# Moving the token-major steps of a two-layer decoder's down projection, and its transposes

## Chip, core and metric

The kernel runs on one core of a Trainium2 chip. The metric is the device time of one launch in microseconds (us). Three executions of the kernel before took 2107.92, 2093.62 and 2107.99 us (median 2107.92). A fourth was profiled and took 2093.35 us. One program is launched, and the host only lays data out.

## What is computed

A decoder trunk of two layers on 256 tokens and a model width of 2048, all in float32:

```python
for l in range(DEPTH):                      # 2 layers
    h = rms_norm(x, norm1_g[l])
    q, k, v, gu, gv = jnp.split(h @ w_in[l], splits, axis=-1)      # 2048 x 5120
    attn = dilated_attention(rotary(q), rotary(k), v)              # 8 heads
    gm = chunked_gmlp(gelu(gu), gelu(gv), ...)                     # 8 groups
    x = x + concat(attn, gm) @ w_out[l]                            # 2048 x 2048
    h2 = rms_norm(x, norm2_g[l])
    x = x + square(relu(h2 @ w_up[l])) @ w_down[l]                 # 2048 x 8192, 8192 x 2048
return rms_norm(x, final_g)
```

## The kernel before

**Data.** The residual stream `x` and the normalised stream `hs` lie channel-major in on-chip memory: channels on the partitions, 16 chunks of 128 channels, 256 tokens along the free axis. Every matrix product is made of three matmuls on float32 values that are split into a high and a low part: high x high, low x high, high x low. A weight tile (128 x 1024, 512 KB) is loaded by SyncE into `raw` (6 buffers), ScalarE makes its high part `hi` (line 152, 7 buffers), VectorE its low part `lo` (line 162, 6 buffers).

**Steps.** The program is a list `steps`, written out in order by the Python code; TensorE runs them in that order. Three kinds of step matter.

- A *channel-major step* (`transposed`, lines 380 to 384) uses one weight tile as the stationary operand and 256 tokens as the moving one: 24 matmuls of 256 columns. In the up projection (`w_up`) four of them finish 256 hidden channels, and `after_up` then runs on VectorE and ScalarE (lines 715, 716, 611, 612). In the down projection two of them finish 256 output channels, and `update` adds them to `x` (line 471). In the last eighth `update` also makes the next norm's inputs: in layer 0 the scaled copies into `hs` (line 269 on ScalarE, 273 on VectorE), in both layers the squares (line 282, added up by line 286), in layer 1 a scaling of `x` (line 290).
- A *token-major step* (`fast`, lines 408 to 411) does part of the down projection's first 512 output channels: tokens are the stationary operand and the weights move. It works by the seven products of a Strassen-Winograd scheme: a `Top` and a `Bottom` tile are loaded, and two `Sums` tiles (upper and lower) are made from them on VectorE (lines 205, 206 and 202, 203) before they are split. It has 42 matmuls of 256 columns, in the order: top (6), bottom (12), upper (12), lower (12). Its stationary operands come from the hidden tile `half` and from `shared`, which holds sums of the hidden tile's blocks (`sums`, lines 729 to 732, and four `parts`, lines 611 and 612).
- An *input step* (`natural`, lines 431 to 433) does part of the input projection with the weights moving: 12 matmuls of 512 columns. Each layer begins with 16 of them.

**Eighths.** The hidden width of 8192 is worked off in eight pieces of 1024. Piece e is made by 16 up steps; the 12 channel-major down steps of piece e-1 follow them; and the two token-major down steps of piece e-1 stand among the up steps of piece e. The loop has a ninth round (`e == 8`) that has no up steps: the two token-major steps stand among its 12 down steps. I call the rounds with token-major steps eighths 1 to 8 and number their steps from 0. Before, the token-major steps stood behind steps 3 and 7 of an eighth (behind steps 2 and 5 in eighth 8). In eighth 1 no down steps come in between: the up steps of piece 1 follow those of piece 0 at once.

**What follows the last token-major step.** Their seven products stay in four PSUM banks through all eight eighths. `combine` (lines 744 to 751, VectorE but for the first) adds them up, two `turn_back` calls transpose the blocks on TensorE (line 760, four transposes each), and each is followed by an `update` of channels 0 to 255 and 256 to 511. In layer 0 these make `hs` chunks 0 to 3, the first that the next layer's first step reads. In layer 1 their squares go into the final norm's sum (line 297 on TensorE sums it over the channels, lines 320 to 331 make its root, line 305 spreads it, line 877 scales the output).

**Order of side work.** `later(delay, cost, fn)` puts work into a first-in first-out queue with the earliest step at which it may run; `now` counts weight tiles, and a token-major step counts as four. After each step `run_queue` runs entries that are due until a budget of 1.2 is spent; `flush` at the end runs what is left. Each step first issues the splits of tiles up to five ahead, then its matmuls, then its `after` work, then one helping of the queue. VectorE and ScalarE run what is issued strictly in that order.

Of the kernel before, what the change touches and what calls it, by code (L numbers as in the profile page):

```python
# [83 lines left out]
def trunk(ctx: ExitStack, tc: tile.TileContext, layout, xT, consts, gains, w, b_sp, w_sp, out):  # L84
# [40 lines left out]
    def aux_bank():  # L125
        return paux.tile([P, 512], F32, name="aux", tag="aux")
# [100 lines left out]
    def later(delay, cost, fn):  # L227

        queue.append((now[0] + delay, cost, fn))
# [109 lines left out]
    steps = []  # L339
# [5 lines left out]
    def collect(fn, *args, **kw):  # L345
        n = len(steps)
        fn(*args, **kw)
        part = steps[n:]
        del steps[n:]
        return part  # L350
# [92 lines left out]
    def from_tiles(tiles, n):  # L443
        return lambda k: tiles[k // n][0][:, k % n, :, :]
# [21 lines left out]
    def update(norm, c, ps, final, last):  # L466

        alone = last and final and c == KC - 2
        for j in range(2) if alone else [slice(0, 2)]:
            xj = x[:, c + j, :] if alone else x[:, c:c + 2, :]  # L470
            vec.tensor_tensor(xj, xj, ps[j][:, 0:S] if alone else pair(ps)[:, j, :], op=OP.add)  # L471
        if final:
            if not last:
                norm.chunks(c)
            norm.square(c, alone)
            if last:
                norm.gain(c)

    def layer(l, n1, n2, n3, last):
# [230 lines left out]
        def after_up(e):  # L710
            def f(c, ps):
                if hid[e][0] is None:
                    new_half(hid[e])
                z = inner[:, c // P:c // P + 2, :]
                vec.tensor_tensor(z, pair(ps), n2.R[:, None, :].to_broadcast([P, 2, S]), op=OP.mult)  # L715
                vec.scalar_tensor_tensor(z, z, 0.0, z, op0=OP.max, op1=OP.mult)  # L716
                to_half(hid[e][0], c // P, z)
                if c == 768:
                    summed[0] = False
                    if e == 0:  # L720
                        new_shared(F32R)
                        sum_parts[0] = shared[0].rearrange("p (k h t) -> p k h t", k=NH, h=2)
                    later(1, 1.5, sums)
            return f
# [16 lines left out]
        def combine():  # L741
            p1, p2, p3, p5, p7, p6, p4 = (banks[n // 2][:, n % 2 * 256:n % 2 * 256 + 256] for n in range(7))
            b1, u, c11, c12, c21, c22 = (blocks[:, n, :] for n in range(6))
            act.activation(b1, p1, AF.Copy)
            vec.tensor_tensor(u, b1, p6, op=OP.add)
            vec.tensor_tensor(c11, b1, p2, op=OP.add)
            vec.tensor_tensor(c22, u, p7, op=OP.add)
            vec.tensor_tensor(u, u, p5, op=OP.add)
            vec.tensor_tensor(c12, u, p3, op=OP.add)
            vec.tensor_tensor(c21, c22, p4, op=OP.subtract)  # L750
            vec.tensor_tensor(c22, c22, p5, op=OP.add)
            later(1, 1.5, lambda: turn_back(0, c11, c21))
            later(1, 1.5, lambda: turn_back(2, c12, c22))

        def turn_back(c, first, second):
            ps = aux_bank()
            for j in range(2):
                for tt, src in enumerate((first, second)):
                    o = j * S + tt * P
                    pe.transpose(ps[:, o:o + P], src[:, j * P:(j + 1) * P], ident)  # L760
            later(0, 1.5, lambda: update(n3, c, ps, True, last))
# [3 lines left out]
        for e in range(9):  # L765
            up, down, quick = [], [], []
            if e < 8:
                up = collect(transposed, "w_up", l, 0, KC, e * 1024, 1024, from_hs, after_up(e))
            if e:
                down = collect(transposed, "w_down", l, (e - 1) * 1024, 8, FAST, D - FAST, from_tiles([hid[e - 1]], NH),  # L770
                               lambda c, ps, e=e: update(n3, (c + FAST) // P, ps, e == 8, last), apart=last and e == 8)
                quick = collect(fast, "w_down", l, (e - 1) * 1024, 0, [hid[e - 1]], banks, e == 1, e == 8,
                                lambda: later(1, 1.5, combine))
            rest = up or down
            n = len(quick) + 1
            for i in range(n):
                steps.extend(rest[len(rest) * i // (n + 1):len(rest) * (i + 1) // (n + 1)] if quick else rest)
                steps.extend(quick[i:i + 1])
            if quick:
                steps.extend(rest[len(rest) * n // (n + 1):])  # L780
            if up:
                steps.extend(down)
        if last:
# [11 lines left out]
    for l in range(DEPTH):  # L795
        layer(l, norms[2 * l], norms[2 * l + 1], norms[2 * l + 2], l == DEPTH - 1)
# [74 lines left out]
    n = norms[-1]  # L871
# [43 lines left out]
```

## Time and profile before

| | |
|---|---|
| profiled execution | 2093.35 us |
| its span on the core | 2091.5 us (1.85 us lie around it) |
| other executions | 2093.62, 2107.92, 2107.99 us |
| TensorE (PE) busy | 2066.8 us, 99% |
| VectorE (DVE) busy | 1464.4 us, 70% |
| ScalarE (ACT) busy | 1008.9 us, 48% |
| DMA engines | 55.6% for the weight queue, 189 GB/s over the span |

In the profile's rows PE is TensorE's matmuls, PEld its weight loads, DVE VectorE, ACT ScalarE. A timeline row gives the start, the duration, the engine, the line, the operation, output and inputs, a count, and in brackets the idle time of the engine ahead of it with what ended it. A matmul's duration (0.28 us) is longer than its distance from the next one, since matmuls overlap; the distance between starts is what counts. A row of the waits gives the engine and line that waited, what it waited for, the total, the count and the longest. A row of windows gives each engine's busy time in a stretch and `PEclk`, the clock that was granted to TensorE as a share of full speed.

### The profile page before, as it was taken

The numbers are of one execution on the slowest core, as the hardware profiler recorded it, in microseconds if no ns is written. First come the engines' busy times: TensorE is split into PE (matmuls) and PEld (weight loads), VectorE is DVE, ScalarE is ACT, GpSimd is POOL, SyncE is SP. The second block draws the span as 40 slices with busy tenths as digits, with TensorE's granted clock in tenths as the row PEclk, the third lists the DMA queues.
The fourth block names the chain that finished last, engine by engine and source line by source line (L and its number), as shares of the span: only waits on it lengthen the run. The fifth ranks groups of instructions, "written<-read, shape, count | busy, mean of one in ns | idle before, by whom it ended". The sixth has DMA issues, their size and how long they took to land. (4 is left out here: it accounts for less than half of the span.)

```text
span 2091.5 us, 40406 instructions
## 1 busy us (share of the span) xinstructions
PE 2066.8 (99%) x17066; PEld 2028.3 (97%) x17066; DVE 1464.4 (70%) x1800; ACT 1008.9 (48%) x1265; POOL 68.7 (3%) x90
## 2 busy tenths in 40 slices
PE   9999999999999999999999999999999999999997
PEld 8998999899999999999989999998999999999997
DVE  7666766777677677776856576667676676777666
ACT  7555454444454444544645554545353444444444
POOL 0002300000000000000000050000000000000000
PEclk9999999999999999999999999999999999999998
DMA  8555555365565655656565556555565655556543
GB/s 320 175 172 177 196 183 191 134 225 190 172 218 178 226 192 169 216 182 201 189 204 172 183 172 197 185 181 173 170 207 177 216 188 178 196 178 216 191 162 111
DMA packets 112118, 395.38 MB, mean 189 GB/s; under 512 B 12352, under 2 KB 16448, under 8 KB 111936
## 3 DMA queue, kind: packets, MB, share of 16 engines
q1 hardware_dynamic: 110800, 389.86, 55.6%
q8 instruction: 133, 2.18, 0.4%
q10 hardware_dynamic: 1136, 2.94, 0.4%
q14 instruction: 49, 0.40, 0.1%
HBM read 390.65 MB, written 2.10 MB: 188 GB/s over the span
## 5 line engine op out<-in xcount | busy, mean ns | idle before, releaser
L152 ACT ACTIVATE hi<-raw 128x1024 fp32r<-128x1024 f32 (+1 forms) x773 | 783.7, 1046 | 420.8 <-PE acc L384 194.5
L162 DVE TENSOR_TENSOR lo<-raw,hi 128x1024 fp32r<-128x1024 f32 (+1 forms) x773 | 907.8, 1211 | 42.0 <-ACT hi L152 25.8
L380 PE MATMUL acc<-hs,hi 128*128 128x256 f32 x2816 | 784.3, 279 | 0.0
L384 PE MATMUL acc<-hs,hi 128*128 128x256 f32 x2816 | 781.8, 278 | 0.0
L382 PE MATMUL acc<-hs,lo 128*128 128x256 f32 x2816 | 781.8, 278 | 0.0
L380 PE MATMUL acc<-half,hi 128*128 128x256 f32 x2048 | 569.5, 278 | 0.0
L382 PE MATMUL acc<-half,lo 128*128 128x256 f32 x2048 | 569.1, 278 | 0.0
L384 PE MATMUL acc<-half,hi 128*128 128x256 f32 x2048 | 569.0, 278 | 0.0
L380 PEld LDWEIGHTS acc<-hs,hi 128*128 128x128 f32 x2816 | 532.3, 189 | 0.4 <-issue 0.2
L382 PEld LDWEIGHTS acc<-hs,lo 128*128 128x128 f32 x2816 | 528.8, 188 | 0.4 <-issue 0.2
L384 PEld LDWEIGHTS acc<-hs,hi 128*128 128x128 f32 x2816 | 528.6, 188 | 0.0
L380 PEld LDWEIGHTS acc<-half,hi 128*128 128x128 f32 x2048 | 387.6, 189 | 0.0
L382 PEld LDWEIGHTS acc<-half,lo 128*128 128x128 f32 x2048 | 384.4, 188 | 0.1
L384 PEld LDWEIGHTS acc<-half,hi 128*128 128x128 f32 x2048 | 384.4, 188 | 0.0
L611 ACT ACTIVATE half<-ar 128x512 fp32r<-128x512 f32 x72 | 45.6, 633 | 323.5 <-DVE ar L716 308.9
L471 DVE TENSOR_TENSOR x<-x,acc 128x512 f32<-128x512 f32 (+1 forms) x113 | 76.7, 680 | 174.6 <-PE acc L384 174.6
L715 DVE TENSOR_TENSOR ar<-acc,nR 128x512 f32<-128x512 f32 x64 | 44.2, 691 | 196.0 <-PE acc L384 196.0
L431 PE MATMUL acc<-hi,hs 128*128 128x512 f32 x256 | 101.4, 396 | 0.5 <-ACT hs L269 0.5
L433 PE MATMUL acc<-hi,hs 128*128 128x512 f32 x256 | 100.8, 394 | 0.0
L432 PE MATMUL acc<-lo,hs 128*128 128x512 f32 x256 | 100.1, 391 | 0.0
L612 DVE TENSOR_TENSOR half<-ar,half 128x512 fp32r<-128x512 f32 x72 | 49.8, 692 | 50.3 <-ACT half L611 50.3
L408 PE MATMUL aux<-hi,shared 128*128 128x256 f32 x256 | 73.4, 287 | 10.4 <-ACT shared L611 10.4
(127 smaller groups left out, 1548.2 us busy)
## 6 DMA issues: line engine op xcount, KB each, us to landing
raw<-in_w SPq DMA_DIRECT2D x731, 512.0 KB, 4.5
raw<-in_w SPq DMA_DIRECT2D x10, 256.0 KB, 5.3
x<-in_xT SPq DMA_DIRECT2D x7, 256.0 KB, 5.6
out<-x SPq DMA_DIRECT2D x7, 256.0 KB, 3.1
shared<-in_b_sp ACTq DMA_DIRECT2D x2, 512.0 KB, 7.0
shared<-in_w_sp ACTq DMA_DIRECT2D x2, 512.0 KB, 8.5
con<-in_consts ACTq DMA_DIRECT2D x1, 512.0 KB, 7.4
x<-in_xT ACTq DMA_DIRECT2D x1, 256.0 KB, 4.2
```

The costliest lines, as they stand in the source:

```text
L152: act.activation(self.h[:, j * m:(j + 1) * m], self.raw[:, j * m:(j + 1) * m], AF.Copy)
L162: vec.tensor_tensor(lo[:, r], self.raw[:, r], self.h[:, r].bitcast(F32), op=OP.subtract)
L380: pe.matmul(o, lhsT=hi, rhs=xs[:, 0, :], start=(k0 + k == 0 and (two or cb == 0)), stop=False, skip_group_check=True)
L382: pe.matmul(o, lhsT=wt.lo[:, k, cb * P:(cb + 1) * P], rhs=xs[:, 0, :], start=False, stop=False, skip_group_check=True)
L384: pe.matmul(o, lhsT=hi, rhs=xs[:, 1, :], start=False, stop=last, skip_group_check=True)
L408: pe.matmul(o, lhsT=xh, rhs=hi, start=(first and p == 0 and k == 0 and n % 2 == 0), stop=False, skip_group_check=True)
L431: pe.matmul(ps, lhsT=xh, rhs=hi, start=(k0 + k == 0), stop=False)
L432: pe.matmul(ps, lhsT=xh, rhs=lo, start=False, stop=False)
L433: pe.matmul(ps, lhsT=xl, rhs=hi, start=False, stop=(k0 + k == KC - 1))
L471: vec.tensor_tensor(xj, xj, ps[j][:, 0:S] if alone else pair(ps)[:, j, :], op=OP.add)
L611: act.activation(t[:, c:c + 2, 0, :], src, AF.Copy)
L612: vec.tensor_tensor(t[:, c:c + 2, 1, :], src, t[:, c:c + 2, 0, :].bitcast(F32), op=OP.subtract)
```

## The change

The two token-major steps now stand ahead of steps 6 and 7 of an eighth, so that one channel-major step lies between them; in eighth 1 they stand ahead of steps 10 and 11. The two `turn_back` calls become due one weight tile later. Matmuls, splits, loads and buffers are the same in kind and number.

```diff
-            later(1, 1.5, lambda: turn_back(0, c11, c21))
-            later(1, 1.5, lambda: turn_back(2, c12, c22))
+            later(2, 1.5, lambda: turn_back(0, c11, c21))
+            later(2, 1.5, lambda: turn_back(2, c12, c22))
...
             rest = up or down
-            n = len(quick) + 1
-            for i in range(n):
-                steps.extend(rest[len(rest) * i // (n + 1):len(rest) * (i + 1) // (n + 1)] if quick else rest)
-                steps.extend(quick[i:i + 1])
-            if quick:
-                steps.extend(rest[len(rest) * n // (n + 1):])
+            at = (10, 11) if e == 1 else (6, 7)
+            for i, one in enumerate(rest):
+                if quick and i in at:
+                    steps.append(quick.pop(0))
+                steps.append(one)
```

VectorE's order in eighth 1, from the last `after_up` of piece 0 on. L175 is the low part of the first token-major step's top tile, L729 to L732 begin the sums of the hidden tile, and L612 with `shared` stores a part of them. Before:

```order
L612 TENSOR_TENSOR half<-ar,half 128x2x256
L175 TENSOR_TENSOR lo<-raw,hi 128x512
L729 TENSOR_TENSOR ar<-ar 128x4x128
L730 TENSOR_TENSOR ar<-ar 128x4x128
L731 TENSOR_TENSOR ar<-ar 128x4x128
L732 TENSOR_TENSOR ar<-ar 128x4x128
L205 TENSOR_TENSOR raw<-raw 128x2x256
L206 TENSOR_TENSOR raw<-raw 128x2x256
L162 TENSOR_TENSOR lo<-raw,hi 128x1024
L612 TENSOR_TENSOR shared<-ar,shared 128x2x256
```

Now, from the same place:

```order
L612 TENSOR_TENSOR shared<-ar,shared 128x2x256
L162 TENSOR_TENSOR lo<-raw,hi 128x1024
L612 TENSOR_TENSOR shared<-ar,shared 128x2x256
L162 TENSOR_TENSOR lo<-raw,hi 128x1024
L175 TENSOR_TENSOR lo<-raw,hi 128x512
L205 TENSOR_TENSOR raw<-raw 128x2x256
L206 TENSOR_TENSOR raw<-raw 128x2x256
```

These are the last two of the four `shared` parts: all four now stand ahead of the first token-major step's splits, where before the splits were issued in between.

VectorE's order at the end of layer 0, from the `update` of down step 9 on. `x<-x,acc` is an update by a channel-major step, `x<-x,aux` one by a transposed block. Before:

```order
L471 TENSOR_TENSOR x<-x,acc 128x512
L273 SCALAR_TENSOR_TENSOR hs<-x,cols,hs 128x256 x2
L286 TENSOR_TENSOR nacc<-nacc,nsq 128x512
L471 TENSOR_TENSOR x<-x,aux 128x512
L273 SCALAR_TENSOR_TENSOR hs<-x,cols,hs 128x256 x2
L286 TENSOR_TENSOR nacc<-nacc,nsq 128x512
L162 TENSOR_TENSOR lo<-raw,hi 128x1024
L471 TENSOR_TENSOR x<-x,aux 128x512
L273 SCALAR_TENSOR_TENSOR hs<-x,cols,hs 128x256 x2
L286 TENSOR_TENSOR nacc<-nacc,nsq 128x512
L162 TENSOR_TENSOR lo<-raw,hi 128x1024
L471 TENSOR_TENSOR x<-x,acc 128x512
```

Now:

```order
L471 TENSOR_TENSOR x<-x,acc 128x512
L273 SCALAR_TENSOR_TENSOR hs<-x,cols,hs 128x256 x2
L286 TENSOR_TENSOR nacc<-nacc,nsq 128x512
L162 TENSOR_TENSOR lo<-raw,hi 128x1024 x2
L471 TENSOR_TENSOR x<-x,acc 128x512
L273 SCALAR_TENSOR_TENSOR hs<-x,cols,hs 128x256 x2
L286 TENSOR_TENSOR nacc<-nacc,nsq 128x512
L471 TENSOR_TENSOR x<-x,aux 128x512
L273 SCALAR_TENSOR_TENSOR hs<-x,cols,hs 128x256 x2
L286 TENSOR_TENSOR nacc<-nacc,nsq 128x512
L471 TENSOR_TENSOR x<-x,aux 128x512
```

Both updates by transposed blocks moved from ahead of the update of down step 11, the layer's last, to behind it.

VectorE's order at the end of layer 1, from the same place on. L321 begins the final norm's root. Before:

```order
L471 TENSOR_TENSOR x<-x,acc 128x512
L286 TENSOR_TENSOR nacc<-nacc,nsq 128x512
L471 TENSOR_TENSOR x<-x,aux 128x512
L286 TENSOR_TENSOR nacc<-nacc,nsq 128x512
L471 TENSOR_TENSOR x<-x,aux 128x512
L286 TENSOR_TENSOR nacc<-nacc,nsq 128x512
L471 TENSOR_TENSOR x<-x,acc 128x256 x2
L321 TENSOR_SCALAR rv<-aux 128x2
```

Now:

```order
L471 TENSOR_TENSOR x<-x,acc 128x512
L286 TENSOR_TENSOR nacc<-nacc,nsq 128x512
L471 TENSOR_TENSOR x<-x,acc 128x256 x2
L471 TENSOR_TENSOR x<-x,aux 128x512
L286 TENSOR_TENSOR nacc<-nacc,nsq 128x512
L471 TENSOR_TENSOR x<-x,aux 128x512
L286 TENSOR_TENSOR nacc<-nacc,nsq 128x512
L321 TENSOR_SCALAR rv<-aux 128x2
```

The update of the last down step (in two halves) moved from behind the two updates by transposed blocks to ahead of them.

## The prediction, as made before the changed kernel ran

> **What bounds the kernel now.** I read the page's first part, then TensorE's waits, then its timeline.
>
> ```profile
> span 2091.5 us, 40406 instructions
> PE 2066.8 (99%) x17066; PEld 2028.3 (97%) x17066; DVE 1464.4 (70%) x1800; ACT 1008.9 (48%) x1265; POOL 68.7 (3%) x90
> ...
> PE aux L408 <- ACT shared L611: 10.4, 2, 5.2
> ...
> PE aux L760 <- DVE ar L750: 1.1, 1, 1.1
> ```
>
> TensorE is never without work but for some 15 us of named waits. The largest is the first token-major step of eighth 1, once in each layer: it waits 5.2 us for `shared`. So the time is made of three things: these waits, the speed of TensorE behind them, and the distance between matmuls everywhere else. The next rows are the starts of that token-major step and of the step behind it, in layer 0 and layer 1, then TensorE's clock.
>
> ```profile
> 388.21 0.28 PE L408 MATMUL aux<-hi,half 128*128 128x256 f32 x1
> ...
> 401.37 0.28 PE L380 MATMUL acc<-hs,hi 128*128 128x256 f32 x1
> ...
> 1417.02 0.28 PE L408 MATMUL aux<-hi,half 128*128 128x256 f32 x1
> ...
> 1429.55 0.28 PE L380 MATMUL acc<-hs,hi 128*128 128x256 f32 x1
> ```
>
> ```profile
> 393.90:400.70 6.80, 5.78 (x25) 5.49 (x26) 6.33 (x7) 5.89 (x8) 0.00 (x0) 0.50 0.53 166
> 1421.40:1428.20 6.80, 4.46 (x19) 4.17 (x20) 6.07 (x8) 5.03 (x7) 0.00 (x0) 0.50 0.48 150
> ```
>
> The two steps last 13.16 and 12.53 us. The second fence's column before the last two is the granted clock: 0.50 for 6.8 us around the end of each wait, so that the wait costs more than its 5.2 us.
>
> The third thing is hidden in the 99%. These are starts of whole runs of matmuls in an eighth of layer 0 and one of layer 1: token-major step, channel-major steps, token-major step, channel-major steps, next token-major step.
>
> ```profile
> 482.92 0.28 PE L408 MATMUL aux<-hi,half 128*128 128x256 f32 x1
> ...
> 487.68 0.28 PE L380 MATMUL acc<-hs,hi 128*128 128x256 f32 x1
> ...
> 498.99 0.28 PE L408 MATMUL aux<-hi,half 128*128 128x256 f32 x1
> ...
> 503.94 0.28 PE L380 MATMUL acc<-hs,hi 128*128 128x256 f32 x1
> ...
> 569.23 0.28 PE L408 MATMUL aux<-hi,half 128*128 128x256 f32 x1
> ```
>
> ```profile
> 1513.05 0.28 PE L408 MATMUL aux<-hi,half 128*128 128x256 f32 x1
> ...
> 1518.00 0.28 PE L380 MATMUL acc<-hs,hi 128*128 128x256 f32 x1
> ...
> 1528.89 0.28 PE L408 MATMUL aux<-hi,half 128*128 128x256 f32 x1
> ...
> 1533.65 0.28 PE L380 MATMUL acc<-hs,hi 128*128 128x256 f32 x1
> ...
> 1601.50 0.28 PE L408 MATMUL aux<-hi,half 128*128 128x256 f32 x1
> ```
>
> In layer 0 the 576 matmuls of the long stretch take 65.29 us, 113.35 ns each, and the 96 between the two token-major steps 11.31 us, 117.8 ns each. In layer 1 it is the other way round: 67.85 us or 117.8 ns in the long stretch, 10.89 us or 113.4 ns between. The same holds in the other eighths. So the distance has two values, narrow and wide, 4.45 ns apart; it is kept until a token-major step ends and is the other one behind it (a token-major step itself runs at the distance that it found: 4.76 or 4.95 us). Up to eighth 1 both layers run narrow. In layer 0 the wide stretch stayed between the two steps; in layer 1 the wait in eighth 1 left the phase turned round, and the long stretches are wide.
>
> **The change, part by part.** The sum is made against the profiled execution's 2093.35 us.
>
> *(1) The wait in eighth 1 goes.* An undisturbed token-major step takes 4.76 us (487.68 - 482.92), so the two cost 8.40 + 7.77 = 16.2 us too much, clock included. Now the first one begins behind ten steps, some 27 us after piece 0, and VectorE's listing has all four parts of `shared` ahead of it: about 20 us of VectorE work, done before. -16.2 us.
>
> *(2) The wide stretches shrink.* Wide matmuls in layer 0: 6 eighths with 96 + 42, eighth 1 with the same, eighth 8 with 72 + 42: 1080, or 4.8 us. In layer 1, from the second step of eighth 1 on: 6 x (576 + 42) + (552 + 42) + 48 = 4350, or 19.4 us. A check: were layer 0 turned round too, the time would be 2093.35 + 19.4 - 4.8 = 2107.95; the other executions shown took 2107.92, 2107.99 and 2093.62. So I read the median as both layers turned round, and the profiled execution as one. With the wait gone, nothing turns the phase in eighth 1, and both layers should keep narrow long stretches, with 24 + 42 wide matmuls an eighth: 16 x 66 = 1056, or 4.7 us. 24.2 - 4.7: -19.5 us. Bounds: nothing, if the phase is turned by something else, to -19.5.
>
> *(3) Steps close together.* A token-major step is much work for VectorE and ScalarE:
>
> ```profile
> 1513.25 0.69 DVE L715 TENSOR_TENSOR ar<-acc,nR 128x512 f32<-128x512 f32 x1 [3.55 <-PE acc L384]
> ...
> 1515.98 4.62 DVE L162 TENSOR_TENSOR lo<-raw,hi 128x1024 fp32r<-128x1024 f32 x4
> 1520.52 0.68 DVE L175 TENSOR_TENSOR lo<-raw,hi 128x512 fp32r<-128x512 f32 x1
> ...
> 1525.16 2.52 DVE L162 TENSOR_TENSOR lo<-raw,hi 128x1024 fp32r<-128x1024 f32 x2
> ```
>
> Its eight VectorE instructions take 7.16 us (1520.52 to 1527.68) against 4.9 us on TensorE; `after_up` takes 2.73 us (1513.25 to 1515.98), a split 1.15. I start at the end of up step 3 in eighths 2 to 7, where the buffers let VectorE be ahead by steps 4, 5 and the first half of the token-major step. Then come `after_up` (2.7), the second half (1.34 + 2.52), step 6's split (1.15) and the second token-major step up to its upper tile (5.9): 13.6 us. TensorE has steps 4 and 5 (5.44), a token-major step (4.76), step 6 (2.83) and 18 matmuls (2.1), and wants that tile at 15.1. So 1.5 us are to spare, and the cost is 0. In eighth 1 the phase to step 7 is the same.
>
> *(4) The end of layer 0.* Here VectorE has more to do than TensorE. VectorE's rows, then ScalarE's copy of `hs` chunk 0, then TensorE's first token-major step of eighth 8 and its first input step of layer 1:
>
> ```profile
> 1015.21 5.76 DVE L162 TENSOR_TENSOR lo<-raw,hi 128x1024 fp32r<-128x1024 f32 x5
> 1020.89 0.41 DVE L745 TENSOR_TENSOR ar<-ar,aux 128x256 f32<-128x256 f32 x1
> ...
> 1023.58 1.22 DVE L162 TENSOR_TENSOR lo<-raw,hi 128x1024 fp32r<-128x1024 f32 x1
> 1024.71 0.68 DVE L471 TENSOR_TENSOR x<-x,acc 128x512 f32<-128x512 f32 x1
> ...
> 1027.50 2.35 DVE L162 TENSOR_TENSOR lo<-raw,hi 128x1024 fp32r<-128x1024 f32 x2
> ...
> 1032.55 0.68 DVE L471 TENSOR_TENSOR x<-x,aux 128x512 f32<-128x512 f32 x1
> ```
>
> ```profile
> 1033.27 0.91 ACT L269 ACTIVATE hs<-x,cols 128x256 fp32r<-128x256 f32 x2 [1.36 <-DVE x L471]
> ```
>
> ```profile
> 998.08 0.28 PE L408 MATMUL aux<-hi,half 128*128 128x256 f32 x1
> ...
> 1035.00 0.39 PE L431 MATMUL acc<-hi,hs 128*128 128x512 f32 x1
> ```
>
> Before, chunk 0 was there at 1033.8 and TensorE began the layer at 1035.0 without a wait: 45.1 us from the start of the eighth (three steps of 2.72 ahead of 998.08). Now the update that makes chunk 0 stands behind that of step 11. From the end of step 5 on VectorE has four updates of 2.79 us (1024.71 to 1027.50), a token-major step's 7.2, one split, the five splits of steps 7 to 11 (5.8), `combine` (2.7) and four splits of the next layer (4.7): 32.6 us, and it starts 1.3 us late, as step 3's update and the first token-major step's second half (6.65) are more than two steps. Chunk 0 follows 1.2 us behind the start of its update (1032.55 to 1033.8): 35.1 us. TensorE's work from there to the end of step 11 is 27.1 us with transposes, and I count three waits within: 0.4 for step 6's split, 0.9 for the second token-major step's upper tile, 1.1 for `combine` at the transposes (there were 1.1 before). At 29.4 it is done, and it idles 5.7 us. The layer starts 16.3 + 35.1 = 51.4 us after the eighth, 6.3 later than before. The clock then falls as in eighth 1, where 5.2 us of idling cost 8.1 on the mean, 2.9 of it at half clock; I take 2.6. +8.9 us. Bounds: +3, if VectorE is not behind (the update of step 11 alone, 2.79, and 1.2 ahead of chunk 0 are then left, less 1.1), to +11.
>
> *(5) The end of layer 1.* VectorE's last updates, ScalarE's squares and scaling, TensorE's sum:
>
> ```profile
> 2073.21 0.68 DVE L471 TENSOR_TENSOR x<-x,aux 128x512 f32<-128x512 f32 x1
> ...
> 2075.20 0.68 DVE L471 TENSOR_TENSOR x<-x,aux 128x512 f32<-128x512 f32 x1
> ...
> 2077.19 0.74 DVE L471 TENSOR_TENSOR x<-x,acc 128x256 f32<-128x256 f32 x2
> ```
>
> ```profile
> 2077.64 0.75 ACT L280 ACTIVATE nsq<-x 128x256 f32<-128x256 f32 x2
> 2078.29 0.89 ACT L290 ACTIVATE x<-x,cols 128x256 f32<-128x256 f32 x2
> ```
>
> ```profile
> 2076.34 0.28 PE L384 MATMUL acc<-half,hi 128*128 128x256 f32 x1
> 2077.33 1.05 PE L297 MATMUL aux<-ones,nacc 128*128 128x1 f32 x8 [0.71 <-DVE nacc L286]
> ```
>
> Before, two updates of 1.99 us each (2073.21, 2075.20, 2077.19) ran under the last matmuls, and the sum began 0.7 us behind them. Now they come last. ScalarE is free 2.1 us after the last matmul (0.1, then 2077.19 to 2079.18), the first update's square and addition are done by 3.4, the second needs 1.99 and its own addition: the sum can begin 5.5 us after the last matmul, +4.8. Its 16 matmuls (1.9 us) then stand behind an idle time that was enough for half clock in eighth 1: +1.5. Together +6.3 us; bounds +4 (two updates) to +8.5. In layer 1 an update lacks the 0.8 us of line 273, VectorE isn't behind, and the transposes' wait for `combine` is gone or absent.
>
> The Trainium skill, page "TensorE: Matmul & The Clock Gate", Part 1, speaks against (4) and (5): it says that an idle window of some 3.4 us takes TensorE's clock to half, and that some 3.4 us of work bring it back. The trace agrees in kind, with 0.50 over 6.8 us. By the page's figures alone the two clock terms would be about 1.7 us each where I take 2.6 and 1.5 (an estimate from that page), 0.7 less in the sum.
>
> Sum: 2093.35 - 16.2 - 19.5 + 8.9 + 6.3 = **2073 us**. By the median of 2107.92 this is 1.7% less, by the lower executions 1.0% less. With the bounds of (4) and (5) it lies between 2065 and 2078.
>
> **Rivals.**
>
> *A. One layer still runs wide.* For it: the new idle stretch at the end of layer 0 is as long as the wait that turned layer 1 round. Against it: between it and eighth 1 lie the transposes and norms of a whole layer, and both layers came to eighth 1 narrow, layer 0 from a cold start. Layer 1 would have its long stretches wide: 17 to 18 us more, 2091; if its 106 channel-major steps ahead of that were wide too (2544 matmuls, 11 us), 2102. Or the second token-major step doesn't turn the phase back at a distance of one step; that costs about the same for each layer it strikes.
>
> *B. The idle stretches aren't there.* If VectorE is on time at both ends, (4) is 3 and (5) is 4: 2065. Against it: the listing, and 32.6 us of VectorE rows against 27.1.
>
> *C. Slower.* The second token-major step's upper tile is late in the 14 eighths of (3). It decides from 1.5 us on, the spare time of the ledger. A wait within a token-major step is what turned the phase before, so it would cost its own length, say 1 us x 14, and leave both layers wide, 2 x 17: 2073 + 48 = 2121. For it: two 7.2 us loads of VectorE within 12.5 us of TensorE. Against it: the ledger.
>
> **How the numbers follow.** The forecast gets 0.70, A 0.18, B 0.08, C 0.04. A difference of under 1% (21 us) is about what a measurement of this kernel can't tell from no change, as its executions lie 14.5 us apart. Against 2107.92 that line is at 2087. The forecast and B are below it, but 0.05 of the forecast goes to "same" for the case that the kernel before is met in its lower executions; A is the same; of C, 0.03 counts as slower (2121 is 0.6% over the median, 1.3% over the lower executions) and 0.01 as the same. Faster 0.73, same 0.24, slower 0.03. The range takes in B at its lower end and the cheaper form of A at its upper: 2064 to 2093; the forecast's own is 2065 to 2078.
>
> **What would show it.** Right: no wait of line 408 for line 611 and no half clock near 390 and 1410 us; 552 or 648 matmuls between two eighths' token-major steps at 113.4 ns in both layers, and 117.8 only in the one step between the two and in the second of them; a wait of some 5 us of line 431 for line 269 at the end of layer 0, with half clock behind it; a wait of line 297 of some 5 us at the end. Wrong: a row of waits for lines 408 to 411 on the splits in eighths 2 to 7 (then C), or long stretches at 117.8 ns in a layer (A).

## The result, and the profile after

Four executions of the changed kernel took 2072.85, 2072.96, 2072.50 and 2072.82 us, median 2072.84. The kernel before took 2107.92, 2093.62, 2107.99 and 2094.19 us beside them, median 2101.06. The ratio on record is 0.9895 with a 95% interval of 0.9846 to 0.9945; the quotient of the medians is 0.9866. The interval is wide because of the kernel before alone: its executions here lie at two levels, some 14 us apart (later runs show a third), those of the changed kernel within 0.5 us. The page's head and TensorE's waits after the change:

```profile
span 2071.1 us, 40400 instructions
PE 2046.6 (99%) x17066; PEld 2008.2 (97%) x17066; DVE 1464.8 (71%) x1800; ACT 1010.8 (49%) x1265; POOL 68.8 (3%) x90
```

```profile
PE acc L431 <- ACT hs L269: 5.5, 2, 5.2
PE aux L297 <- DVE nacc L286: 5.0, 1, 5.0
...
PE aux L760 <- DVE ar L750: 1.1, 2, 0.7
...
PE aux L410 <- DVE lo L162: 0.6, 1, 0.6
PE acc L382 <- DVE lo L162: 0.3, 1, 0.3
```

The row of line 408 waiting for line 611 (10.4 us) is gone; two waits of 5 us at the layers' ends have come, of about the same sum. TensorE is "99% busy" as before, and 20.2 us of busy time are gone for the same 17066 instructions: the matmuls stand closer, and fewer of them run at half clock. An eighth of layer 1, by the same starts as in the prediction (token-major step, channel-major step, token-major step, long stretch, next token-major step):

```profile
1506.46 0.28 PE L408 MATMUL aux<-hi,half 128*128 128x256 f32 x1
...
1511.22 0.28 PE L380 MATMUL acc<-hs,hi 128*128 128x256 f32 x1
...
1514.05 0.28 PE L408 MATMUL aux<-hi,half 128*128 128x256 f32 x1
...
1519.00 0.28 PE L380 MATMUL acc<-hs,hi 128*128 128x256 f32 x1
...
1592.45 0.28 PE L408 MATMUL aux<-hi,half 128*128 128x256 f32 x1
```

The 648 matmuls of the long stretch take 73.45 us, 113.35 ns each: narrow, in layer 1 as in layer 0. The 24 between the two steps take 2.83 us, 117.9 ns each: wide, as is the second token-major step (4.95 us for 42). The end of layer 0, from the last matmul of its step 11, and the clock around it:

```profile
1024.98 0.28 PE L384 MATMUL acc<-half,hi 128*128 128x256 f32 x1
1030.50 0.79 PE L431 MATMUL acc<-hi,hs 128*128 128x512 f32 x1 [5.24 <-ACT hs L269]
```

```profile
1030.00:1037.00 7.00, 6.50 (x17) 5.17 (x18) 5.87 (x9) 5.64 (x9) 1.77 (x1) 0.56 0.42 156
```

The idle stretch is there, 5.24 us, and a clock of 0.56 behind it. The end of layer 1, in the chain of work that ended last (start, duration, what), from the last matmul on:

```profile
2050.18 0.13 PE acc L384
2050.34 0.43 DVE x L471
2050.79 0.42 ACT nsq L280
2051.21 0.80 ACT x L290 x2
2052.00 0.53 ACT nsq L282
2052.55 0.69 DVE nacc L286
2053.25 0.61 DVE x L471
2053.88 0.64 ACT nsq L282
2054.54 0.70 DVE nacc L286
2055.28 3.58 PE aux L297 x16
```

It follows the order that the listing showed: the last step's halves first, then one update by a transposed block with its square and addition, then the other. The sum begins 5.1 us behind the last matmul's start and takes 3.58 us, where it took 1.96 before.

### The profile page after: what moved, and what is told of

It reads as the page before. It is cut to its first block, busy times and chain, and to the rows that moved or that the text cites. A ratio compares the mean times of both kernels' runs of the same rounds, so it can differ in the third digit from the quotient of the medians.

```text
span 2071.1 us, 40400 instructions
## 1 busy us (share of the span) xinstructions
PE 2046.6 (99%) x17066; PEld 2008.2 (97%) x17066; DVE 1464.8 (71%) x1800; ACT 1010.8 (49%) x1265; POOL 68.8 (3%) x90
## 4 chain that ended last, share of the span: by engine, by line
PE 96%; DVE 2%; ACT 1%; issue 0%; DMA 0%; ACTq 0%; DVEq 0%
PE acc L382 26%; PE acc L384 26%; PE acc L380 26%; PE acc L431 3%; PE acc L433 3%; PE acc L432 3%; PE aux L408 2%; PE aux L410 2%; PE aux L411 2%; DVE lo L162 1%; PE aux L657 0%; PE aux L559 0%; PE aux L601 0%; PE aux L297 0%; DVE x L471 0%
## 5 line engine op out<-in xcount | busy, mean ns | idle before, releaser
L612 DVE TENSOR_TENSOR half<-ar,half 128x512 fp32r<-128x512 f32 x72 | 49.8, 692 | 50.8 <-ACT half L611 50.8
L269 ACT ACTIVATE hs<-x,cols 128x256 fp32r<-128x256 f32 x64 | 29.0, 501 | 92.6 <-DVE x L471 91.4
```

What stands on the lines that cost most here:

```text
L612: vec.tensor_tensor(t[:, c:c + 2, 1, :], src, t[:, c:c + 2, 0, :].bitcast(F32), op=OP.subtract)
```

## The experiments

Each kernel ran beside the kernel before on the same chip. The theory: a token-major step turns TensorE's distance to its other value, the wait in eighth 1 left it to chance which stretches come out narrow and which wide, and the ends cost what their order costs. The rival: standing one step apart is itself what keeps the distance narrow.

### Eighth 1 alone

```diff
-            at = (10, 11) if e == 1 else (6, 7)
+            at = (10, 11) if e == 1 else (4, 8) if e < 8 else (3, 6)
...
-            later(2, 1.5, lambda: turn_back(0, c11, c21))
-            later(2, 1.5, lambda: turn_back(2, c12, c22))
+            later(1, 1.5, lambda: turn_back(0, c11, c21))
+            later(1, 1.5, lambda: turn_back(2, c12, c22))
```

> Theory (the wait in eighth 1 cost its own 16.2 us and left the distance between matmuls turned round; where the two token-major steps stand in the later eighths matters little): eighth 1 as in the change, all else as before. No wait of 5.2 us, long stretches narrow (113.4 ns) in both layers, wide (117.8 ns) only in the four steps between the two token-major steps and in the second of them: 2 x (66 + 6 x 138 + 114) = 2016 wide matmuls, 9.0 us, where the profiled execution before had 24.2. 2093.35 - 16.2 - 15.2 = 2062 us in every execution, and no idle stretch of 5 us at the layers' ends. Rival (standing close together is what keeps the long stretches narrow): layer 1's long stretches are still wide at 117.8 ns, and only the wait is saved: 2077 us, or 2092 with both layers wide.

It took 2062.15 us (2061.99 to 2062.28; ratio 0.9828, interval 0.9748 to 0.9909). Its waits, and a long stretch and the steps ahead of it in eighth 2:

```profile
PE aux L305 <- DVE nr L331: 1.2, 1, 1.2
...
PE aux L297 <- DVE nacc L286: 0.7, 1, 0.7
```

```profile
479.02 0.28 PE L380 MATMUL acc<-hs,hi 128*128 128x256 f32 x1
...
490.33 0.28 PE L408 MATMUL aux<-hi,half 128*128 128x256 f32 x1
...
495.28 0.28 PE L380 MATMUL acc<-hs,hi 128*128 128x256 f32 x1
...
560.58 0.28 PE L408 MATMUL aux<-hi,half 128*128 128x256 f32 x1
```

The 96 matmuls between the steps are wide (11.31 us), the 576 behind them narrow (65.30 us), with the steps four apart. The theory's number and its pattern held; the rival's didn't. All of the gain and more lies in eighth 1; the other two edits together cost 2072.84 - 2062.15 = 10.7 us.

### Eighth 1 back in its place

```diff
-            at = (10, 11) if e == 1 else (6, 7)
+            at = (4, 8) if e == 1 else (6, 7)
```

> Eighths 2 to 8 and the transposes as in the change, eighth 1 behind steps 3 and 7 as before. Theory: the wait is back, +16.2 us, and leaves each layer's distance at narrow or wide by chance: 2089 us with none turned round, about 2107 with one layer, 2125 with both; executions differ by steps of some 17 us, and in the profile a layer that is turned round has its 648 matmuls between the eighths at 117.8 ns. Rival (standing close together keeps the stretches narrow): 2089 us in every execution, all long stretches at 113.4 ns.

Executions took 2107.01, 2125.63, 2127.04 and 2125.47 us (ratio 1.011, interval 1.0029 to 1.0191). The profiled one was the first. The 624 matmuls from eighth 1 to eighth 2 in layer 0, then in layer 1:

```profile
415.94 0.28 PE L380 MATMUL acc<-hs,hi 128*128 128x256 f32 x1
...
489.43 0.28 PE L408 MATMUL aux<-hi,half 128*128 128x256 f32 x1
```

```profile
1469.98 0.28 PE L380 MATMUL acc<-hs,hi 128*128 128x256 f32 x1
...
1540.71 0.28 PE L408 MATMUL aux<-hi,half 128*128 128x256 f32 x1
```

73.49 us or 117.8 ns in layer 0, 70.73 us or 113.35 ns in layer 1. In this execution it was layer 0 that came out turned round, in the profiled one of before layer 1. So the wait leaves a layer turned round or not, and steps close together don't put it right. With them, a turned layer costs more (18.5 us from level to level), as the long stretches are longer.

### Eighth 8 early

```diff
-            at = (10, 11) if e == 1 else (6, 7)
+            at = (10, 11) if e == 1 else (6, 7) if e < 8 else (3, 4)
```

> The change, but with the token-major steps of eighth 8 ahead of its steps 3 and 4. Theory (the two idle stretches at the layers' ends come from the order, since the updates by transposed blocks stand behind the last down step's): both updates stand ahead of it again, the waits of line 431 for line 269 (5.2 us) and of line 297 for line 286 (5.0 us) go to under 1 us, and with them the half clock behind them (2.6 and 1.7 us): 2072.8 - 14 = 2058 to 2059 us. Rival (VectorE is too loaded by two token-major steps one step apart, wherever they stand): the idle stretches shrink by half at most, 2065 us or more.

It took 2055.34 us (2055.05 to 2055.55; ratio 0.9796, interval 0.9729 to 0.9863), the best version of this study: 17.5 us under the changed kernel.

```profile
PE aux L305 <- DVE nr L331: 1.2, 1, 1.2
PE aux L837 <- DVE warm L833: 1.1, 1, 1.1
PE acc L431 <- ACT hs L269: 0.5, 1, 0.5
PE acc L382 <- DVE lo L162: 0.3, 1, 0.3
```

TensorE's waits sum to 3.1 us against 14.8: the transposes' (1.1 us) and the upper tile's in eighth 8 (0.6 us) went as well, which the expectation left out. With 4.4 us of clock (layer 1's first 48 matmuls take 10.99 us where they took 13.68, the final sum 3.04 where it took 4.78) and 0.5 us in line 305's matmuls (0.71 for 1.24) that makes 16.6 of the 17.5. VectorE's work is the same; where the two steps stand, and so what is queued behind them, made the ends late.

### One token-major step left out

```diff
                 sums_ready()
+                if row0 == 1024 and p == 1:
+                    return
```

> The change without the 42 matmuls of the second token-major step of eighth 2, in both layers (its tiles are still loaded and split). Theory (each token-major step that TensorE runs turns the distance to its other value, wherever it stands): wide from the first token-major step of eighth 2 on, the long stretches of eighths 2 to 7 at 117.8 ns in both layers, some 4300 wide matmuls a layer instead of 528, +16.8 us a layer against 4.9 us less work: 2096 us. Rival (the distance belongs to the place between the two steps, or to what VectorE and ScalarE do there): long stretches stay at 113.4 ns, 2063 us.

It took 2073.04 us in one execution: neither. Without 4.95 us of matmuls TensorE caught up with the splits, and in eighth 2 of both layers it waited, the first time within two steps:

```profile
PE acc L380 <- ACT hi L152: 1.5, 1, 1.5
PE acc L382 <- DVE lo L162: 1.1, 1, 1.1
```

Behind those waits the granted clock was 0.50 for some 3.4 us, and then the distance was narrow, in both layers. The run doesn't tell the theories apart, since a wait set the distance anew; it shows that in this stretch TensorE has less than 4.95 us to spare on VectorE and ScalarE.

### The same 42 matmuls in the other form

```diff
+                    if row0 == 1024 and p == 1:
+                        for k in range(2):
+                            hi, lo = (t[:, k, cols][:, 0:P] for t in (b.hi, b.lo))
+                            for wt, i in ((hi, 0), (lo, 0), (hi, 1)):
+                                pe.matmul(o, lhsT=wt, rhs=hs[:, 2 * n + k, i, :], start=False, stop=False,
+                                          skip_group_check=True)
+                        continue
                     for k in range(2):
```

> The change, but the second token-major step of eighth 2 runs its 42 matmuls in the channel-major form in both layers (weights stationary, tokens moving; its part of the output is then not the reference's). TensorE's time, VectorE's and ScalarE's work and the place are as in the change. Theory (it is the form of a token-major step, tokens stationary and weights moving, that turns the distance): nothing turns it back in eighth 2, the long stretches of eighths 2 to 7 run at 117.8 ns in both layers, some 4340 wide matmuls a layer instead of 528: 2072.85 + 2 x 17 = 2107 us. Rival (42 more matmuls of any form turn it, since 42 leaves another remainder than 24): narrow as in the change, 2073 us. If a wait sets the distance anew, it shows as a row of waits.

It took 2105.89 us in one execution. The stretch between that step and eighth 3's first token-major step:

```profile
492.62 0.28 PE L380 MATMUL acc<-hs,hi 128*128 128x256 f32 x1
...
568.94 0.28 PE L415 MATMUL aux<-hi,half 128*128 128x256 f32 x1
```

76.32 us for 648 matmuls, 117.8 ns each: wide, and so are the long stretches of every following eighth in both layers. Place, time, count, output banks and the other engines' work are the changed kernel's; the form alone differs. That is the test that the run before failed to be.

### Other counts: 40, 41 and 36

```diff
+                        if n == 2 and k == 1:
+                            continue
```

> The change with 40 matmuls instead of 42 in each token-major step (for one of the seven products, the low x high and high x low matmuls of one chunk are left out, so a small part of its precision). Theory (the form of the step turns the distance): the same stretches wide as in the change, 32 matmuls fewer in all: 2072.85 - 3.6 = 2069 us. Rival (the count of 42 turns it: 42 is no multiple of four, 24 and 40 are): nothing turns the distance, no wide stretch at all, 2069 - 4.7 = 2064.5 us.

```diff
+                        if n == 2 and k == 1:
+                            pe.matmul(o, lhsT=xh, rhs=lo, start=False, stop=False, skip_group_check=True)
+                            continue
```

> The change with 41 matmuls in each token-major step (one high x low matmul left out). Theory (the form of the step): the same stretches wide, 2071 us. Rival (the count modulo four): another pattern of wide stretches than with 42, 40 or 44; with an odd count the two values would come back only after four steps, that is after two eighths.

```diff
-                    for k in range(2):
+                    for k in range(1 if n in (2, 3) else 2):
```

> The change with 36 matmuls in each token-major step: of two of the seven products one of two chunks is left out whole (so that part of the output lacks them), three matmuls each. With 40 the way back from wide to narrow failed, with 41 and 42 it didn't. If a count that is a multiple of four fails, the distance stays wide from the first token-major step on: 2107 - 7 = 2100 us. If it was the broken group of three that failed, 36 turns back like 42: 2072.85 - 10.9 = 2062 us, or somewhat more where VectorE then is the later one.

With 40 it took 2107.32 us, against both expectations. The channel-major stretch behind eighth 1's second step:

```profile
416.85 0.28 PE L380 MATMUL acc<-hs,hi 128*128 128x256 f32 x1
...
481.86 0.28 PE L408 MATMUL aux<-hi,half 128*128 128x256 f32 x1
```

65.01 us for 552 matmuls, 117.8 ns. The first step of 40 turned narrow to wide like one of 42, the second left it wide, and so did every later one. With 41 it took 2068.53 us, with the pattern of the changed kernel but for the 72 matmuls ahead of the transposes, which are wide in both layers; in layer 1 they follow a step that took 4.87 us where the others took 4.83, a delay of 0.04 us. The time is 2.5 us less than I gave it. The 32 token-major steps lose 32 matmuls (17034 for 17066), 3.7 us, and I had taken off half of that (for 40 and 36 as well, which changes none of the readings); and half clock ahead of layer 1 lasted 3.4 us where it lasts 6.8 in the changed kernel, which is worth 1.1 us. With 36 it took 2073.25 us: layer 0 had the pattern of 42, so a multiple of four isn't the cause; layer 1 was turned round from its eighth 1 on. There the second step began, the long stretch began, and the next eighth began at

```profile
1428.62 0.28 PE L408 MATMUL aux<-hi,half 128*128 128x256 f32 x1
...
1433.00 0.28 PE L380 MATMUL acc<-hs,hi 128*128 128x256 f32 x1
...
1498.01 0.28 PE L408 MATMUL aux<-hi,half 128*128 128x256 f32 x1
```

The step took 4.38 us where the others of 36 took 4.24, so it was held up for 0.14 us, too short for a row among the waits; the 552 matmuls behind it are wide (65.01 us). What in a step of 40 fails to turn the distance back stays open.

### The transposes back

```diff
-            later(2, 1.5, lambda: turn_back(0, c11, c21))
-            later(2, 1.5, lambda: turn_back(2, c12, c22))
+            later(1, 1.5, lambda: turn_back(0, c11, c21))
+            later(1, 1.5, lambda: turn_back(2, c12, c22))
```

> The change with the two transposes due one weight tile later as before (the third edit undone). Theory (VectorE is late with combine, so that earlier transposes wait for it, and the idle stretches at the layers' ends come from the updates' place): the first update by transposed blocks stands ahead of step 11's again, the second still behind. In layer 0 the wait at the transposes grows by about a step (2.7 us), the wait of line 431 falls from 5.2 to some 2.5 us, too short for half clock (-2.6 us): 2.6 us less there. In layer 1 one of the two updates is left behind step 11's, so the sum waits some 3.0 us instead of 5.0, and the transposes wait some 1 to 2 us more. Together 2068 to 2071 us. Rival (the later transposes were worth their wait): 2073 us or more.

It took 2075.92 us (2074.89 to 2076.62), 3.1 more than the changed kernel: the expectation missed, the rival's direction held.

```profile
PE acc L431 <- ACT hs L269: 4.6, 2, 3.3
PE aux L760 <- DVE ar L746: 3.8, 2, 2.1
PE aux L297 <- DVE nacc L286: 3.0, 1, 3.0
PE aux L760 <- DVE ar L750: 2.4, 2, 1.2
```

The waits at the ends shrank as expected, from 10.5 to 7.6 us, but those at the transposes grew from 1.1 to 6.2, as `combine` itself was late for its first block (line 746) and its second. In layer 0 the two waits of 2.1 and 1.2 us, with one transpose between them, were followed by a step of 24 matmuls that took 5.15 us, half clock as behind a wait of 5 us. And the wait of 3.3 us ahead of layer 1, which I had called too short for half clock, had it behind it too: the granted clock was 0.50 from 1038.3 to 1041.7 us. So the third edit was worth its 3 us where eighth 8's steps stand late.

### No step between

Base: eighth 8 early.

```diff
-                if quick and i in at:
+                while quick and i == at[0 if e < 8 else 2 - len(quick)]:
                     steps.append(quick.pop(0))
```

> As the version with eighth 8 early, but with no step between the two token-major steps of eighths 1 to 7 (both ahead of step 6, in eighth 1 of step 10). Theory: 24 wide matmuls fewer in each of 14 eighths (-1.5 us). The ledger of the prediction gave VectorE 1.5 us to spare with one step (2.8 us on TensorE, 1.15 on VectorE) between; without it the upper tile is 0.2 us late in each of them: rows of waits of lines 408 to 411 for line 162, some 3 us in all: 2055 to 2058 us. Rival (a wait within a token-major step, however short, turns the distance the other way): long stretches wide in some eighths, 2065 to 2090 us.

Executions took 2067.93, 2068.33, 2063.12 and 2063.44 us: over the theory's 2058, with the wide stretches in some eighths that the rival named. In layer 1 these are the pair of eighth 3 (its start, the first and the third matmul of the second step's upper tile, its end), the pair of eighth 4 (start and end) and the start of eighth 5's:

```profile
1585.47 0.28 PE L408 MATMUL aux<-hi,half 128*128 128x256 f32 x1
...
1592.27 0.28 PE L408 MATMUL aux<-hi,shared 128*128 128x256 f32 x1
...
1592.87 0.28 PE L411 MATMUL aux<-hi,shared 128*128 128x256 f32 x1
...
1595.46 0.28 PE L380 MATMUL acc<-hs,hi 128*128 128x256 f32 x1
...
1674.60 0.28 PE L408 MATMUL aux<-hi,half 128*128 128x256 f32 x1
...
1684.50 0.28 PE L380 MATMUL acc<-hs,hi 128*128 128x256 f32 x1
...
1760.67 0.28 PE L408 MATMUL aux<-hi,half 128*128 128x256 f32 x1
```

In the first pair 60 matmuls take 6.80 us, 113.35 ns each: the distance stays narrow across the border between the two steps. Then the upper tile's low part is late. Two distances take 0.60 us where narrow ones take 0.23, so VectorE is late by 0.37 us, where the ledger had 0.2. The other 22 matmuls are wide, and so are the 672 behind the pair (79.14 us). The second pair starts wide, meets no delay and stays wide through all its 84 matmuls (9.90 us); behind it 672 matmuls take 76.17 us, narrow. So two token-major steps in a row turn the distance once, where the channel-major form comes back, and not once each. The expectation had this wrong, as it counted on the second step to turn the distance back. By the same rule a narrow pair without delay would leave a wide stretch behind it; no such pair is in the trace. All 12 pairs that started narrow had the delay. Behind nine of them the stretch is narrow, behind three, all in layer 1, it is wide. So a delay of a third of a microsecond within a token-major step left the distance to chance, and instead of saving 1.5 us the version cost 8 to 13.

### The order of the moving tiles

Base: eighth 8 early.

```diff
-                        pe.matmul(o, lhsT=xh, rhs=hi, start=(first and p == 0 and k == 0 and n % 2 == 0), stop=False,
+                        pe.matmul(o, lhsT=xh, rhs=lo, start=(first and p == 0 and k == 0 and n % 2 == 0), stop=False,
...
-                        pe.matmul(o, lhsT=xh, rhs=lo, start=False, stop=False, skip_group_check=True)
+                        pe.matmul(o, lhsT=xh, rhs=hi, start=False, stop=False, skip_group_check=True)
```

> As the version with eighth 8 early, with the first two matmuls of each group of three in a token-major step exchanged (high x low ahead of high x high). Theory (tokens stationary and weights moving turn the distance, in whatever order): the same wide stretches, 2055.3 us. Rival (the order of the moving tiles does it): no wide stretch, 2051 us, or wide ones that stay, some 2090 us.

It took 2055.53 us in one execution, with the wide stretches in the same places: the order of the moving tiles doesn't matter.

## Why the prediction was right

The profiled execution took 2072.85 us against 2073. It isn't a balance of errors. Between the two profiled executions the time up to eighth 8 of layer 0 changed by -10.6 us, that eighth by +6.1, the start of layer 1 at half clock by +2.5, the rest up to eighth 8 of layer 1 by -24.3, and what follows by +5.9; the terms of the sum, sorted by the same stages, give -10.6, +6.1, +2.6, -24.4 and +5.9. By its terms:

- **(1) and (2), the wait and the wide stretches.** Right, mechanism and size. Eighth 1 alone, with neither of the costs of (4) and (5), took 2062.15 us where the same two terms, with its 2016 wide matmuls, gave 2062. The kernel before was executed 31 times beside these kernels: 4 at 2077.4 to 2079.0, 12 at 2092.3 to 2095.4, 15 at 2107.3 to 2108.6 us. I read these as no, one and two layers turned round. Only the execution of 2093.35 us was profiled and shows its one layer; for the others it rests on arithmetic. The prediction's check gave 2107.95 for two, and the same arithmetic gives 2078.8 for none, a level that no execution had shown yet. That the wait is what leaves it to chance is shown by the levels' return with the wait (eighth 1 back) and their absence without.
- **(3), steps close together.** Right: no wait of the token-major steps in eighths 1 to 7 of the changed kernel. The ledger's spare time of 1.5 us held roughly where it could be tried: with 2.83 us on TensorE and 1.15 us on VectorE less the upper tile was 0.37 us late, where the ledger gives 0.2.
- **(4), the end of layer 0.** Right, with sizes a little over: 5.24 us of idling for 5.7, 0.3, 0.6 and 0.7 us at the split, the upper tile and the transposes for 0.4, 0.9 and 1.1. The clock fell as expected and cost 2.5 us for 2.6 (layer 1's first 48 matmuls take 13.68 us, before they took 11.18).
- **(5), the end of layer 1.** Right: the sum waits 5.0 us and takes 3.58 us, 1.6 us more than before, for 1.5. One detail was wrong: the transposes wait 0.3 us in layer 1 too, where I had none.

Together (4), (5) and the 960 wide matmuls (4.3 us) that the later eighths save by standing close should have made the changed kernel 8.9 + 6.3 - 4.3 = 10.9 us slower than eighth 1 alone; it is 10.7. How much faster the change looks depends on which levels of the kernel before are met: 1.7% by the highest, 1.0% by the middle one.

On the clock: the Trainium skill, page "TensorE: Matmul & The Clock Gate", Part 1, gives an idle window of about 3.4 us ahead of half clock. The runs agree for idle stretches of 5.0 to 5.2 us. Half clock also came behind less: waits of 2.1 and 1.2 us with a transpose between, one wait of 3.3 us (both with the transposes back), and waits of 1.5 and 1.1 us with one matmul between (one token-major step left out); there the measurement decides. On the distance: the Trainium skill, same page, "Back-to-back issue gap", has a formula for the gap of a matmul by itself, which gives 256 / 2.4 + 2.5 = 109 ns here (an estimate from that page). The traces have two values, 113.35 and 117.8, and they decide.

Rival A didn't come: the 5 us of idling at the end of layer 0 left layer 1 narrow in the profiled execution, and the times of the other three leave no room for a wide layer. It was a sound fear, though: the delay of 0.14 us in the run with 36 turned layer 1 round from inside a token-major step. C's mechanism, a late upper tile that can turn the long stretches wide, was shown by the version with no step between, at 0.37 us of delay.

Not shown: what in TensorE keeps the two distances apart, and why a step of 40 doesn't turn it back. The runs say that a run of matmuls with stationary tokens and moving weights turns it where it ends, that waits and delays can, and that the order of the moving tiles doesn't matter. The two forms differ in one more thing that no run separates: in a token-major step a stationary tile serves two matmuls in a row.

## What to carry to other kernels

A TensorE that reads 99% busy can still be 4% slower in one stretch than in another: divide long runs of equal matmuls by their count, and compare the stretches before looking for waits. Executions that fall on a few levels can point to a state that a rare wait leaves to chance, as here; look for the wait first, since its own length may be the smaller part of its price. And when steps move by a place or two, follow what is queued behind them to the end of the stage: here an order that was right in the middle put two updates behind the last step at both ends, and three places earlier were worth 17 us.

## What the runs showed of the hardware that I had not expected

TensorE's distance between the 256-column matmuls of the up and down projections took two values, 113.35 and 117.8 ns, at full granted clock, each kept over 648 matmuls and more. It turned from one to the other behind a run of token-major matmuls, of 42 as of 84; of the runs of 40, each layer's first did so and the later ones didn't. A delay of 0.14 us within a token-major step was enough to leave the long stretches at the other one for the rest of the layer's eighths, in one execution. Waits of 2.1 and 1.2 us, neither of them long, brought half clock when they followed each other with one transpose between. Behind an idle stretch of 5.2 us half clock lasted 6.8 us in the changed kernel and 3.4 us in the run with 41.
